# The state-to-output tables of a state-space layer, built beside the experts and no longer beside the linear attention

## Chip, cores and metric

One core of a Trainium2 chip. The metric is the time of one execution in device microseconds. Engines: TensorE (PE: matmuls; PEld: its weight loads), VectorE (DVE), ScalarE (ACT), GpSimd (POOL), SyncE (SP, which here only issues transfers). Sixteen DMA engines serve the queues of SP, ACT and POOL.

## What is computed

A first block (attention, an mLSTM, then a mixture of 32 experts, two per token) and a second block of two layers (gated linear attention, then a state-space layer "S5"), on 256 tokens of width 1024. The part that matters here is the output side of S5: a complex linear recurrence per group, of which the real part of C times the state is read.

```python
def step(carry, u_i):
    ...
    acum_r, acum_i, x_r, x_i = lax.associative_scan(_linrec_combine, (a_r, a_i, bu_re, bu_im), axis=1)
    ...
    y = jnp.einsum('bcgp,ghp->bcgh', x_r, c_re) - jnp.einsum('bcgp,ghp->bcgh', x_i, c_im)
```

The kernel takes four time steps at once. So it needs, beside C itself, the products C·A, C·A², C·A³ and C·A⁴ for each of 128 groups with 64 states: these are the state-to-output tables. They depend on weights alone.

## The kernel before

**Stages in time.** Modulation and first block to about 235 us; experts (`moe`) to 772; linear attention (`gla`) to 1070; S5 (`s5`) to the end.

**Experts.** `moe` runs eight calls of `quad`, four experts each. A call takes 24 tiles of weights of 1 MB (`w1`, `w3`, `w2`) from memory, through a pool of 5 and one of 2 buffers. `quad` yields after each tile, and `beside` steps two other jobs in between, at fixed rates: `kvs` (keys and values of the memory attention for both layers: 16 blocks of 1 MB) and `tables`.

**High and low halves.** Most dense products take each 1 MB block of fp32 weights in two halves. For each, ACT writes the rounded `whi` (L267), and another engine subtracts it from the raw block to give `wlo` (L268). In the experts that is POOL (`self.spread = 2`), later DVE. The raw buffer is free for SP's next load (L262) only when both are through with it.

**Tables.** `tables` first runs `s5_setup` (DVE: powers of A; POOL: clears of a few tiles, and zeros to parts of `tab3` in memory). Then it takes eight blocks `jb`: `s5_powers` makes B-side powers on DVE (24 products and sums of 128x128, lines 1285 to 1290) and copies C into block-diagonal tiles on POOL (L1304, L1306); one block later `s5_table` multiplies them on TensorE and POOL stores the result to `tab3` in four transfers (L1325).

**State-to-output tables.** `s5_out` loads C (`raw`, L1331), negates its imaginary part (L1335), and makes four complex products in turn, each from the one before: 24 elementwise instructions of 128x128 on POOL (lines 1339 to 1344). The result `t2` is stored to `tab2` in memory (L1346), from where S5 reads it long after, about 1300 us. In the trace `t2` and `s_t2` are shown as `s_t`, `tab2` and `tab3` as `tab`. It is called eight times in `gla`, in the loop over output blocks.

**Order.** Each engine works through its own queue in order. The queue isn't in program order: when the kernel is built, a planner walks through it with estimated durations, and gives each engine what is ready, earlier in the program first. `tc.issue_after(x)` keeps what is traced under it behind `x` on its engine. A tile of a pool has a name and a number of buffers; a new tile of that name waits until the last user of the old one is done. `s_tmp`, a 128x128 scratch tile, has one buffer in the pool of the tables (used by `s5_powers`), and one in the pool that `s5_out` used in `gla`.

Of the kernel before, what the change touches and what calls it, by code (L numbers as in the profile page):

```python
# [181 lines left out]
def bc(ap, n):  # L182

    return ap[:, None, :].to_broadcast([ap.shape[0], n, ap.shape[1]])
# [23 lines left out]
class Kern:  # L208
# [822 lines left out]
    def moe(self):  # L1031
        tc = self.tc
        with tc.tile_pool(name="moe", bufs=1) as R:
            W = tc.alloc_tile_pool(name="quad", bufs=2)
            self.lam = self.t(R, [128, 192], "lam")
            self.nc.gpsimd.dma_start(self.lam, self.io["slam"])
            steps = self.route(R)
            next(steps)
            xg = self.gather(0, W, "at")
            for _ in steps:  # L1040
                pass
            self.spread = 2
            for _ in range(4 * KV_EARLY):
                next(self.kvs)
            self.psum_banks(m=2, A=4, ps=2)
            self.kvtag = "ps"
            self.next = xg, None
            beside(self.quad(0, W), [(self.kvs, KV_FIRST)])
            self.pre.release()
            P = tc.alloc_tile_pool(name="aux", bufs=1, side="right")  # L1050
            self.kvpool, self.kvbufs = P, 4
            tables = self.tables(P)
            next(tables)
            for q in range(1, 8):
                if q == 7:
                    for _ in itertools.chain(self.kvs, tables):
                        pass
                    P.release()
                    self.overflow()
                    self.G = tc.alloc_tile_pool(name="gh", bufs=1, side="right")  # L1060
                beside(self.quad(q, W), [] if q == 7 else [(self.kvs, KV_LATER), (tables, TABLES)])
            W.release()
# [3 lines left out]
    def tables(self, P):  # L1066

        self.s5_setup(P)
        yield
        pair = [None, None]  # L1070
        for jb in range(9):
            if jb < 8:
                pair[jb % 2] = yield from self.s5_powers(P, jb)
            if jb:
                yield from self.s5_table(P, jb - 1, pair[(jb - 1) % 2])


    def memory(self, P):
# [91 lines left out]
    def s5_setup(self, P):  # L1170
# [4 lines left out]
        def f(name):  # L1175
            return self.t(P, [128, 64], "s_" + name)
# [13 lines left out]
        dt, a, b = f("dt"), f("a"), f("b")  # L1190
# [57 lines left out]
        for b in range(2):  # L1248
            p = self.psum()
# [10 lines left out]
        for x in self.bdC[0] + self.bdC[1]:  # L1260
            nc.gpsimd.memset(x, 0.0)

        zero = self.t(P, [48, 128], "s_zero")
        nc.gpsimd.memset(zero, 0.0)
        for k in range(3):
            n = 16 * (3 - k)
# [60 lines left out]
    def s5_out(self, P, jb):  # L1327

        nc, e = self.nc, self.nc.gpsimd
        raw = self.t(P, [128, 2, 8, 16], "s_raw", bufs=2)  # L1330
        e.dma_start(raw, self.io["sbc"][jb][:, 2:4])  # L1331
        t2 = self.t(P, [128, 8, 64, 2], "s_t2", bufs=2)
        tmp = self.t(P, [128, 8, 16], "s_tmp")
        A = [self.s5ab[:, i, 8 * jb:8 * jb + 8, None].to_broadcast([128, 8, 16]) for i in range(2)]
        e.tensor_scalar(raw[:, 1], raw[:, 1], -1.0, None, op0=OP.mult)  # L1335
        y = (raw[:, 0], raw[:, 1])
        for k in range(4):
            o = tuple(t2[:, :, 16 * k:16 * k + 16, i] for i in range(2))
            e.tensor_mul(o[0], y[0], A[0])
            e.tensor_mul(tmp, y[1], A[1])  # L1340
            e.tensor_add(o[0], o[0], tmp)
            e.tensor_mul(o[1], y[1], A[0])
            e.tensor_mul(tmp, y[0], A[1])
            e.tensor_sub(o[1], o[1], tmp)
            y = o
        e.dma_start(self.tab2[jb], t2.rearrange("p j s i -> p j (s i)"))  # L1346
# [19 lines left out]
    def gla(self):  # L1366
        nc, io, tc = self.nc, self.io, self.tc
        G0 = self.G
        with tc.tile_pool(name="g", bufs=1) as P, tc.tile_pool(name="gw", bufs=2) as W, \
# [27 lines left out]
            start = nc.gpsimd.tensor_mul(mg[:, 0:2, 0], rc, r1c)  # L1397
# [28 lines left out]
            a = self.t(P, [128, 4, T], "gA")  # L1426
# [87 lines left out]
            late = []  # L1514
            for b in range(12):
                ps = self.dense_t(io["gz"][b], h)
                if b < 8:
                    with tc.issue_after(start.ins):
                        self.s5_out(O, b)
                zt = self.t(W, [128, 2, T], "zt")  # L1520
                nc.vector.tensor_mul(zt, ps, bc(r, 2))
                nc.scalar.activation(zt, zt, AF.Silu)
                fs = (2 * b, 2 * b + 1)
                late.append([(f, self.gated(W, oh[f // 4][:, f % 4] if f < 16 else xa[:, f - 16], zt[:, f % 2])) for f in fs])
                for b_ in range(max(b - 1, 0), 12 if b == 11 else b):
                    for w, (f, y) in zip(self.halves(io["wo0"][b_]), late[b_]):
                        self.wout(acc, w, y, f == 0, f == 23)
                    if b == 10:
                        self.mark = self.last
# [258 lines left out]
```

## Time and profile before

| | |
|---|---|
| median of 3 runs (lowest to highest) | 1544.42 us (1543.29 to 1549.2) |
| the profiled execution | 1552.19 us, span 1550.4 us |
| busy: PE, DVE, ACT, POOL | 1353.3, 768.4, 549.9, 402.5 us |
| bytes moved by the DMA engines | 406.47 MB, mean 262 GB/s |
| POOL's own DMA queue | 9.54 MB, 1.8% of 16 engines' span |

The profile is one execution. Times are microseconds from the start of its span. "Busy" is the time in which an engine executes; "DMA share" is the mean busy share of the sixteen DMA engines, PEclk the TensorE clock that was granted, as a part of full speed. An arrow in a row reads "out <- in", and an arrow in brackets names what ended the wait.

### The profile page before, as it was taken

What the parts mean: (1) busy time and instruction counts of PE and PEld (TensorE: products, weight loads), DVE (VectorE), ACT (ScalarE), POOL (GpSimd) and SP (SyncE); (2) the same over time, 40 slices, a digit from 0 to 9 for tenths busy, and PEclk for the clock granted to TensorE, in tenths of its full rate; (3) what the DMA queues carried; (4) which work ended last, traced back from release to release, by engine and by line L of the source; (5) the groups of instructions that cost most, each with busy time, mean ns of one, the idle gap of its engine ahead of it and who ended that gap; (6) DMA issues with size and microseconds to landing.
All of it is one profiled execution on the core that took longest, in us unless ns stands there. A gap on an engine that the chain in (4) does not pass through costs nothing.

```text
span 1550.4 us, 25869 instructions
## 1 busy us (share of the span) xinstructions
PE 1353.3 (87%) x10632; PEld 1078.5 (70%) x10632; DVE 768.4 (50%) x1526; ACT 549.9 (35%) x861; POOL 402.5 (26%) x461
## 2 busy tenths in 40 slices
PE   6999989878897789766698999999789768899998
PEld 3777886434454455411198899999778767899998
DVE  2766464621143200100177765667646799755453
ACT  3754553122111212110145446545122354444443
POOL 0031032221332221100069970002334334330001
PEclk8999999998798989887888999999999989999998
DMA  9777666999999999998974444556686333565540
GB/s 376 263 257 263 259 227 253 373 407 418 413 401 395 421 417 403 418 420 366 401 259 161 148 155 170 182 187 205 192 220 186 121 113 109 181 201 184 174 160 28
DMA packets 84235, 406.47 MB, mean 262 GB/s; under 512 B 25088, under 2 KB 26672, under 8 KB 40080
## 3 DMA queue, kind: packets, MB, share of 16 engines
q1 hardware_dynamic: 67856, 386.04, 66.3%
q10 hardware_dynamic: 12720, 9.18, 1.8%
q0 software_dynamic: 3536, 9.54, 1.8%
q8 instruction: 86, 1.41, 0.4%
q14 instruction: 37, 0.30, 0.1%
HBM read 388.70 MB, written 16.02 MB: 261 GB/s over the span
## 4 chain that ended last, share of the span: by engine, by line
PE 33%; DVE 10%; DMA 9%; issue 1%; POOL 1%; ACT 0%; SPq 0%; DVEq 0%; POOLq 0%; ACTq 0%
PE ps L280 19%; PE acc L280 8%; DMA sm<-md 4%; DMA w<-in_w 3%; PE st L280 3%; DVE sc L1665 2%; DVE Xs L1668 2%; PE at L280 1%; DVE sc L1667 1%; DVE sc L1666 1%; PE A L280 1%; DMA yy<-yd 1%; PE m L280 0%; DVE zt L1576 0%; DVE wlo L268 0%
## 5 line engine op out<-in xcount | busy, mean ns | idle before, releaser
L267 ACT ACTIVATE whi<-w 128x1024 fp32r<-128x1024 f32 x252 | 263.1, 1054 | 341.9 <-PE ps L280 250.5
L268 DVE TENSOR_TENSOR wlo<-w,whi 128x1024 fp32r<-128x1024 f32 x198 | 258.2, 1307 | 150.8 <-ACT whi L267 150.3
L280 PE MATMUL ps<-hh,whi 128*128 128x256 f32 x928 | 278.2, 300 | 15.0 <-DVE zt L1576 6.2
L280 PE MATMUL ps<-hl,whi 128*128 128x256 f32 x928 | 271.2, 292 | 0.7 <-DVE hl L1541 0.4
L280 PE MATMUL ps<-hh,wlo 128*128 128x256 f32 x928 | 270.5, 292 | 0.0
L280 PEld LDWEIGHTS ps<-hh,whi 128*128 128x128 f32 x928 | 183.0, 197 | 23.5 <-issue 11.1
L268 POOL TENSOR_TENSOR wlo<-w,whi 128x1024 fp32r<-128x1024 f32 x54 | 129.0, 2398 | 255.5 <-ACT whi L267 255.4
L280 PEld LDWEIGHTS ps<-hl,whi 128*128 128x128 f32 x928 | 183.7, 198 | 2.0 <-DVE hl L1541 0.5
L280 PEld LDWEIGHTS ps<-hh,wlo 128*128 128x128 f32 x928 | 183.2, 198 | 1.6 <-issue 0.7
L280 PE MATMUL A<-w,xg 128*32 128x512 f32 x984 | 140.9, 674 | 34.1 <-DMA w<-in_w 33.2
L280 PE MATMUL acc<-gyl,whi 128*128 128x256 f32 x384 | 108.8, 284 | 1.6 <-DVE gyl L268 1.6
L280 PE MATMUL acc<-gyh,wlo 128*128 128x256 f32 x384 | 108.7, 283 | 0.0
L280 PE MATMUL acc<-gyh,whi 128*128 128x256 f32 x384 | 108.2, 283 | 0.0
L933 DVE SCALAR_TENSOR_TENSOR xT<-m,mod,xT 128x256 f32<-128x256 f32 x64 | 27.8, 480 | 146.7 <-PE m L280 146.7
L280 PE MATMUL A<-w,gT 128*32 128x512 f32 x512 | 74.9, 680 | 25.2 <-DMA w<-in_w 18.0
L280 PEld LDWEIGHTS A<-w,xg 128*32 128x32 f32 x984 | 23.8, 114 | 101.8 <-DMA w<-in_w 71.9
L280 PEld LDWEIGHTS acc<-gyl,whi 128*128 128x128 f32 x384 | 72.9, 190 | 2.4 <-DVE gyl L268 2.1
L280 PEld LDWEIGHTS acc<-gyh,wlo 128*128 128x128 f32 x384 | 73.2, 191 | 0.2 <-issue 0.2
L280 PEld LDWEIGHTS acc<-gyh,whi 128*128 128x128 f32 x384 | 72.6, 190 | 0.2 <-issue 0.2
L959 DVE TENSOR_TENSOR g<-g,A 128x512 f32<-128x512 f32 x8 | 5.5, 688 | 135.0 <-PE A L280 135.0
L280 PE MATMUL ps<-wlo,hh 128*128 128x256 f32 x192 | 55.9, 291 | 4.6 <-DVE wlo L268 4.6
L280 PE MATMUL ps<-whi,mh 128*128 128x256 f32 x128 | 43.3, 339 | 15.7 <-ACT whi L267 15.7
(577 smaller groups left out, 2791.0 us busy)
## 6 DMA issues: line engine op xcount, KB each, us to landing
w<-in_w SPq DMA_DIRECT2D x187, 1024.0 KB, 11.0
w<-in_wada SPq DMA_DIRECT2D x24, 1024.0 KB, 7.0
w<-in_wo SPq DMA_DIRECT2D x24, 1024.0 KB, 5.1
w<-in_sglu SPq DMA_DIRECT2D x16, 1024.0 KB, 4.9
w<-in_gz SPq DMA_DIRECT2D x12, 1024.0 KB, 4.9
w<-in_sz SPq DMA_DIRECT2D x12, 1024.0 KB, 4.9
w<-in_win SPq DMA_DIRECT2D x10, 1024.0 KB, 10.0
w<-in_xk SPq DMA_DIRECT2D x8, 1024.0 KB, 13.0
```

The lines of the kernel that those rows point to most:

```text
L267: self.nc.scalar.activation(hi, src, AF.Copy)
L268: (eng or self.nc.vector).tensor_sub(lo, src, hi.bitcast(F32))
L280: self.nc.tensor.matmul(ps, l, r, start=start, stop=stop, **kw)
L933: self.nc.vector.scalar_tensor_tensor(self.xT[:, f], pc[:, T * c:T * c + T], self.m(5)[:, f:f + 1], self.xT[:, f], op0=OP.mult, op1=OP.add)
L959: nc.vector.tensor_mul(g1, g1, p3)
L1665: nc.vector.tensor_mul(t1, Xs[:, :, c - 1], a4[0])
L1666: nc.vector.tensor_mul(t2, Xs[:, :, c - 1, ::-1], a4[1])
L1667: nc.vector.tensor_add(t1, t1, Xs[:, :, c])
L1668: nc.vector.tensor_add(Xs[:, :, c], t1, t2)
```

## The change

`s5_out` is called from `tables`, for block `jb - 1` directly behind that block's `s5_table`, and no longer from `gla`. It then uses the pool of the tables. The tiles `raw` and `t2` have one buffer each and no longer two, `raw` has a name of its own (`s_rawc`), and `s_tmp` is shared with `s5_powers`. The cleared tile of `s5_setup` takes its place in `s_tmp`'s buffer.

```diff
@@ tables
             if jb:
                 yield from self.s5_table(P, jb - 1, pair[(jb - 1) % 2])
+                self.s5_out(P, jb - 1)
@@ s5_setup
-        zero = self.t(P, [48, 128], "s_zero")
+        zero = self.t(P, [128, 8, 16], "s_tmp").rearrange("p a b -> p (a b)")[:48]
         nc.gpsimd.memset(zero, 0.0)
@@ s5_out
-        raw = self.t(P, [128, 2, 8, 16], "s_raw", bufs=2)
+        raw = self.t(P, [128, 2, 8, 16], "s_rawc")
         e.dma_start(raw, self.io["sbc"][jb][:, 2:4])
-        t2 = self.t(P, [128, 8, 64, 2], "s_t2", bufs=2)
+        t2 = self.t(P, [128, 8, 64, 2], "s_t2")
         tmp = self.t(P, [128, 8, 16], "s_tmp")
@@ gla
                 ps = self.dense_t(io["gz"][b], h)
-                if b < 8:
-                    with tc.issue_after(start.ins):
-                        self.s5_out(O, b)
```

## Rows read from the trace of the kernel before

**Rows 1.** The page's busy tenths: DMA, the span in 40 slices.

```profile
...
DMA  9777666999999999998974444556686333565540
...
```

**Rows 2.** Experts by stretch: span, busy PE, PEld, DVE, ACT, POOL, PEclk, DMA share.

```profile
...
300.00:320.00 20.00, 16.64 (x120) 7.78 (x112) 4.02 (x9) 7.02 (x16) 0.28 (x1) 1.00 0.88 356
...
520.00:540.00 20.00, 17.16 (x138) 8.98 (x134) 8.51 (x29) 4.84 (x11) 4.53 (x9) 1.00 1.01 421
...
680.00:705.00 25.00, 17.65 (x80) 4.66 (x84) 2.44 (x5) 1.19 (x2) 0.17 (x2) 0.66 0.82 334
...
```

**Rows 3.** Chain of waits, end of the experts: start us, us, what.

```profile
...
734.81 15.54 DMA w<-in_w
...
```

**Rows 4.** Linear attention by stretch, same columns.

```profile
...
785.00:818.00 33.00, 32.49 (x251) 31.17 (x251) 21.34 (x30) 12.20 (x14) 26.14 (x46) 0.94 0.65 234
818.00:839.00 21.00, 16.50 (x140) 16.29 (x138) 19.25 (x26) 15.32 (x19) 20.27 (x29) 0.95 0.24 82
839.00:875.00 36.00, 35.41 (x319) 34.62 (x320) 21.49 (x39) 14.47 (x23) 34.54 (x60) 0.94 0.60 212
875.00:893.00 18.00, 14.88 (x73) 11.79 (x72) 17.95 (x34) 7.92 (x18) 17.11 (x36) 1.00 0.27 96
893.00:930.00 37.00, 36.64 (x283) 36.24 (x284) 23.28 (x31) 16.20 (x19) 27.65 (x50) 0.95 0.47 161
...
```

**Rows 5.** DMA queues, 785 to 950 us: queue, packets, MB, share of 16 engines.

```profile
...
q0 software_dynamic: 1536, 5.24, 8.4%
...
```

**Rows 6.** DMA queues and issues (KB, us to landing), 262 to 600 us.

```profile
...
q1 hardware_dynamic: 17746, 129.24, 92.8%
q0 software_dynamic: 1952, 4.20, 4.1%
...
w<-in_w SPq DMA_DIRECT2D x112, 1024.0 KB, 10.8
...
tab<-s_zero POOLq DMA_DIRECT2D x2, 192.0 KB, 7.8
...
```

**Rows 7.** Timeline of DVE, start of the tables: start us, us, instruction.

```profile
...
284.00 0.28 DVE L1289 TENSOR_TENSOR s_tmp<-s_pe,a 128x128 f32<-128x128 f32 x1
284.31 2.32 DVE L1290 TENSOR_TENSOR s_pe<-s_pe,s_tmp 128x128 f32<-128x128 f32 x1
...
```

**Rows 8.** Timeline of POOL, the same place.

```profile
...
284.05 4.81 POOL L268 TENSOR_TENSOR wlo<-w,whi 128x1024 fp32r<-128x1024 f32 x2
...
```

**Rows 9.** Timeline of DVE, linear attention.

```profile
...
830.49 1.49 DVE L1444 SCALAR_TENSOR_TENSOR gqk<-gqk,gG 128x1024 f32<-128x1024 f32 x1
...
833.25 0.45 DVE L1448 TENSOR_SCALAR gqx<-gqk,gG 128x64 f32<-128x64 f32 x1
...
834.94 0.24 DVE L1450 TENSOR_SCALAR gqx<-gqk,gG 128x64 f32<-128x64 f32 x1
...
837.54 5.56 DVE L268 TENSOR_TENSOR wlo<-w,whi 128x1024 fp32r<-128x1024 f32 x4
...
880.15 2.30 DVE L1501 SCALAR_TENSOR_TENSOR gqk<-gqk,vec,gro 128x256 f32<-128x256 f32 x4
...
```

**Rows 10.** DVE by line and shape, 990 to 1070 us: busy, mean ns.

```profile
...
L268 DVE TENSOR_TENSOR wlo<-w,whi 128x1024 fp32r<-128x1024 f32 x28 | 34.3, 1225 | 26.0 <-ACT whi L267 26.0
...
L1360 DVE TENSOR_TENSOR gy<-hf,zt 128x256 f32<-128x256 f32 x8 | 3.0, 420 | 0.0
...
```

**Rows 11.** Timeline of DVE, third table's powers.

```profile
...
335.67 0.29 DVE L1285 TENSOR_TENSOR s_pe<-s_raw,s_co 128x128 f32<-128x128 f32 x1 [19.68 <-PE ps L280]
...
341.70 0.29 DVE L1286 TENSOR_TENSOR s_tmp<-s_raw,s_co 128x128 f32<-128x128 f32 x1
...
```

**Rows 12.** Timeline of POOL, the same table.

```profile
...
340.11 0.58 POOL L1278 DMA_DIRECT2D s_raw<-in_sbc  x1
353.69 4.67 POOL L268 TENSOR_TENSOR wlo<-w,whi 128x1024 fp32r<-128x1024 f32 x2 [13.00 <-ACT whi L267]
...
```

**Rows 13.** Waits of SP's queue, 262 to 700 us: total us, times, longest.

```profile
...
SPq L262 <- POOL wlo L268: 68.0, 12, 7.4
...
```

## Prediction, made before the change was run

> **What bounds the kernel now.** I read the busy tenths of the span first, then tables of stretches, then the waits and queues of the two stages that the change touches. The strip of transfers [rows 1] stands at its ceiling from slice 7 to slice 19 (some 270 to 770 us): these are the experts. The table of stretches says the same in numbers [rows 2]: between 300 and 600 us the DMA share is 1.01, while TensorE is busy 17 of 20 us. Two stretches fall short, 300 to 320 (0.88) and 680 to 705 (0.82). At the end of the stage the chain of waits is made of weight transfers, one of 15.5 us alone [rows 3]. So the experts last as long as their bytes need on 16 engines, and a byte added there is paid in time, unless it falls in one of the gaps.
>
> The linear attention (785 to 1070 us) is the other way round. Transfers take half of the engines or less, and TensorE is busy nearly all the time [rows 4]. It has two stretches of its own kind: 818 to 839 and 875 to 893, where DVE is busy 19.25 of 21 and 17.95 of 18 us and TensorE waits. In these DVE sets the pace, and POOL is full with `s5_out` beside it. Idle time of TensorE from 785 to 930, over the five rows: 0.5 + 4.5 + 0.6 + 3.1 + 0.4 = 9.1 us. That is all that a faster DVE can give back there.
>
> **What the change moves.** Eight calls of `s5_out`, each a load of 128 KB, 25 elementwise instructions on POOL and a store of 512 KB. POOL is busy 26.1 + 20.3 + 34.5 + 17.1 + 27.7 = 125.7 us in those five rows, nearly all of it this: 15.7 us a call. All of it goes to the experts.
>
> *Transfers.* 8 x (128 + 512) KB = 5.24 MB, the whole of POOL's queue in the linear attention: 8.4% of the engines over 165 us, 13.9 us of all sixteen [rows 5]. There the engines have room, so leaving costs and gives nothing. In the experts the shares of the queues already add up to the ceiling (92.8 and 4.1% for the two largest in rows 6), and these 13.9 us come on top. Bounds: at the rate of the full stage (421 GB/s, 520 to 540 in rows 2) 12.4 us; at the rate of what POOL's queue moves there now, 4.20 MB in 4.1% of 338 us, or 303 GB/s, 17.3 us [rows 6]. Those are smaller pieces, so I keep the time measured for these very transfers: **+13.9 us**.
>
> *DVE in the linear attention.* POOL and DVE get in each other's way when both read two operands from SBUF. Early in the experts a DVE product takes 0.28 us, the next 2.32 us: a POOL subtraction of 2.4 us began at 284.05 [rows 7, 8]. `s5_out` does this in small pieces. In the two DVE stretches [rows 9] a 1024-wide instruction with two inputs takes 1.4 us (5.56 for four; 1.49 alone), against 1.225 where POOL is idle [rows 10]: 11 of them, 0.17 each, 1.9 us. Twelve `gqx` scalings run from 833.25 to 837.54, 4.3 us; at the shortest of them, 0.24, they would need 2.9: 1.4 us. Twelve normalisations of the heads take 0.575 (2.30 for four), against 0.42 for a product of that width: 1.9 us. Together **-5.2 us**, all in stretches where TensorE waits for DVE. Bounds: nothing, if ScalarE or TensorE ends the wait next; 9.1 us, TensorE's whole idle time.
>
> The Trainium skill ("SBUF — State Buffer", the bandwidth-pool section) puts it as an exclusive lock: the one that starts second waits for the whole instruction of the other. The 2.32 us agree; the 0.17 us do not look like a whole POOL instruction each time. By the rule 23 two-input DVE instructions would each win back up to one POOL instruction, which is more than TensorE's idle time; what that makes of the time is the second rival below.
>
> *POOL and DVE in the experts.* `s_tmp` has one buffer. The trace shows how it is passed on: in the third call of `s5_powers` DVE works from 335.67, after table matmuls, and at 341.70 has begun the next call's first product into `s_tmp` [rows 11], though the rest of that call comes a table later. With `s5_out` in between, the planner, which takes what is ready and stands earlier in the program, must alternate: powers, out, powers, out. So one `s5_out` falls into each table's period of some 31 us, and they don't pile up. It can start at 341.7. The next POOL work after the table's own is a pair of subtractions (the low halves of the memory's key or value weights) at 353.7, 13.0 us after the issue before it [rows 12]. A call of 15.7 us, less without DVE beside it, ends up to 3 us too late. Behind it wait the two subtractions, the matmuls that need them, and SP's next load, which needs their source buffer: SP has waited 68 us for POOL in 12 places already [rows 13], without a gap in the transfers. What hides it: a load takes 10.8 us from issue to landing [rows 6] and so some four are always under way. I cost it at nothing; without that cover it is 8 x 3 = 24 us. DVE's first product of the next call also waits for `s_tmp`, and with it what stands behind it on DVE (expert gating, gathers, combines). It is issued late enough by the plan if the plan's times hold; same cover.
>
> The cleared tile, now in `s_tmp`'s buffer, holds back the first `s5_powers` until its transfers land (7.8 us, rows 6), once: nothing, by the same cover, 7.8 without it. Single buffers for the raw table and the result cost nothing, since a period is longer than load, 15.7 us and store.
>
> **Sum.** 13.9 - 5.2 = +8.7 us. The profiled execution took 1552.2 us (span 1550.4), 7.8 above the median of the runs shown, so it would become 1560.9, and the median 1544.4 becomes **1553**. With the bounds of the two terms: 12.4 - 9.1 = +3.3 to 17.3 - 0 = +17.3, so 1548 to 1562.
>
> **Rivals.**
> 1. *POOL becomes late.* If the planned order puts a whole `s5_out` ahead of the subtractions or of DVE work that TensorE needs, each costs what exceeds the cover: 15.7 - 10.8 = 4.9 us, eight times 39, on top of 8.7: 1592. It decides from the point where a subtraction comes over 10.8 us late. For: SP already waits for POOL [rows 13]. Against: the 13.0 us gap nearly holds a call.
> 2. *The lock gives back more.* All of TensorE's 9.1 us returns: 13.9 - 9.1 = +4.8, 1549. For: rows 7 and 8. Against: the small excess of rows 9 over 10.
> 3. *The transfers are hidden anyway* (the other side). If writes to memory run beside the reads, or fall into the gaps of 300 to 320 and 680 to 705, only the gain stays: -5.2, 1539, and with all of TensorE's idle time 1535. For: the two gaps hold 2.4 + 4.5 = 6.9 us. Against: the share of 1.01, and that `s5_out` would run between 300 and 600, mostly where there is no gap.
>
> **Chances.** Forecast 0.55, rival 1 0.18, rival 2 0.15, rival 3 0.12. About 0.5%, 7.7 us, is what a measurement of this kernel can tell from no change: beyond 1552 is slower, below 1537 faster. The forecast's range has a little over half beyond 1552: slower 0.36 + 0.18 = 0.54. Same: 0.19 + 0.15 + half of rival 3 = 0.40. Faster: the rest of rival 3, 0.06. The range: below 1543 lies most of rival 3, above 1575 most of rival 1, some 2 in 10 together, so 1543 to 1575.
>
> **What would show it.** Right: the experts' end (now 772) about 14 us later, at an unchanged DMA share near 1.0; POOL empty from 785 to 1070; the stretch 785 to 930 about 5 us shorter, its 1024-wide DVE instructions near 1.23 us; one `s5_out` behind each table, 25 instructions in 13 to 16 us. Wrong: new idle time of TensorE behind POOL's subtractions, or DVE standing at `s_tmp<-s_raw` for many us, with the DMA share well under 1 between 300 and 600 (rival 1); an expert stage no longer than before (rival 3); or several `s5_out` calls in one period. The step I trust least is the costless wait at `s_tmp`: the order on POOL and DVE is the planner's, and the trace of before can't show it.

## The result, and the profile after

The changed kernel takes 1601.67 us (median of four, 1600.53 to 1607.47) against 1545.29 for the kernel before on the same chip: 56.4 us more, a ratio of 1.0369 with a 95% interval of 1.0337 to 1.0402. The forecast was 1553; the first rival had 1592.

**Where the time is.** By the chain of waits, the first dense block of the linear attention starts at 776.82 us before and 840.40 after (+63.6). Its last block ends at 1070.35 before, and after at 1114.97 + 11.52 = 1126.49, so the linear attention takes 286.1 us where it took 293.5 (-7.4). The state-space layer behind it takes 479.2, before 480.05. Together +55.3, the difference of the two spans. Everything was lost in the experts.

The page's busy tenths after, first POOL, then DMA [rows 1]:

```profile
...
POOL 0041032533555544110000000000434433320001
...
DMA  9776657989998977999995425455777423474540
...
```

POOL's digits in slices 7 to 15 are 3 to 5 (on the page of before 1 to 3), and none stands in the linear attention (slices 21 to 27). The strip of transfers, before a row of nines from slice 7 to 19 with one 8, now has 8 in slices 8 and 12 and 7 in 14 and 15, all among the slices in which POOL is busier, and is whole again once POOL has next to nothing left to do. The tables of stretches say it in numbers. Columns as in [rows 2]; the experts and the linear attention of the kernel before:

```profile
262.00:776.80 514.80, 409.66 (x2756) 210.41 (x2749) 121.63 (x387) 89.19 (x168) 102.72 (x117) 0.86 0.99 403
776.80:1070.35 293.55, 284.32 (x2232) 276.22 (x2233) 195.11 (x295) 146.24 (x205) 126.10 (x218) 0.97 0.52 181
```

and the same of the kernel after, with two stretches of 20 us inside the experts:

```profile
262.00:840.40 578.40, 422.71 (x2769) 215.95 (x2761) 118.94 (x387) 89.46 (x168) 192.34 (x333) 0.81 0.92 368
300.00:320.00 20.00, 13.53 (x69) 7.09 (x67) 1.88 (x6) 1.72 (x4) 11.17 (x27) 0.75 0.88 347
600.00:620.00 20.00, 9.09 (x49) 6.23 (x50) 0.00 (x0) 0.00 (x0) 12.34 (x21) 0.57 0.37 138
840.40:1126.50 286.10, 283.01 (x2251) 274.88 (x2251) 186.47 (x300) 148.13 (x210) 1.75 (x5) 0.98 0.49 170
```

Before, the sixteen transfer engines taken together stood idle for 1% of 514.8 us, 5 us. After it is 8% of 578.4, 46 us: 41 us of the 63.6 are added idle time of the transfer engines. The other 22 are more busy time, of which the moved transfers make 13.8. That number is from POOL's queue in the table of DMA queues: 2.5% of 547 us before (230 to 777), 4.5% of 610 us after (230 to 840).

```profile
q0 software_dynamic: 3488, 9.44, 4.5%
```

About 8 us of busy time are left over; shares of two digits leave some 3 us open on either side of them.

**What POOL does at a table.** The timeline of POOL after, from the load of a table's raw block (the answer to [rows 12]):

```profile
355.84 0.56 POOL L1279 DMA_DIRECT2D s_raw<-in_sbc  x1
357.46 0.40 POOL L1341 TENSOR_TENSOR s_tmp<-s_rawc,a 128x128 f32<-128x128 f32 x1 [1.06 <-DVE s_pe L1291]
...
368.15 0.60 POOL L1347 DMA_DIRECT2D tab<-s_t  x1 [0.30 <-POOL s_t L1345]
374.33 0.40 POOL L1340 TENSOR_TENSOR s_t<-s_rawc,a 128x128 f32<-128x128 f32 x1 [5.58 <-DMA tab<-s_t]
374.69 0.39 POOL L1343 TENSOR_TENSOR s_t<-s_rawc,a 128x128 f32<-128x128 f32 x1
375.06 4.67 POOL L268 TENSOR_TENSOR wlo<-w,whi 128x1024 fp32r<-128x1024 f32 x2
```

Read the last four lines. A call of `s5_out` ends with its store at 368.15. Directly behind it in POOL's queue stand two products, not of this call but of the next one: they write the result tile `s_t`, which has one buffer, so they wait for the store to land (5.58 us). Only behind them come the subtractions that make `wlo`. These start 17.6 us after the call's first product into `s_tmp` (357.46), and 19.2 us after the load's issue, where before it was 13.6. The last two calls run one after the other:

```profile
589.57 0.62 POOL L1347 DMA_DIRECT2D tab<-s_t  x1 [0.30 <-POOL s_t L1345]
...
597.83 0.40 POOL L1340 TENSOR_TENSOR s_t<-s_rawc,a 128x128 f32<-128x128 f32 x1 [6.97 <-DMA tab<-s_t]
...
607.89 0.60 POOL L1347 DMA_DIRECT2D tab<-s_t  x1 [0.30 <-POOL s_t L1345]
608.50 4.69 POOL L268 TENSOR_TENSOR wlo<-w,whi 128x1024 fp32r<-128x1024 f32 x2
```

and TensorE stands until the subtraction is done, as its timeline shows:

```profile
610.91 0.58 PE L280 MATMUL ps<-wlo,mh 128*128 128x256 f32 x1 [20.91 <-POOL wlo L268]
```

This is the stretch 600 to 620 above: TensorE 9 of 20 us, DMA share 0.37. The matmuls wait for `wlo`, those of the experts stand behind them in TensorE's queue, their weight buffers don't come free, and SP can't issue the next loads.

**What DVE does at a table.** The timeline of DVE after, at the call that began at 357.46 on POOL:

```profile
367.89 0.29 DVE L1287 TENSOR_TENSOR s_tmp<-s_raw,s_co 128x128 f32<-128x128 f32 x1 [10.51 <-POOL s_t L1345]
368.10 0.68 DVE L959 TENSOR_TENSOR g<-g,A 128x512 f32<-128x512 f32 x1
```

and TensorE's:

```profile
368.83 0.90 PE L962 MATMUL m<-c_ident,g 128*128 128x128 f32 x3 [12.96 <-DVE g L959]
```

DVE stands for the whole call, with the first product of the next powers, at the one scratch tile. Right behind that product is `g`, the experts' gated activation, which TensorE needs next: it waits 12.96 us. The same pair stood there before; the row behind the one in [rows 11] is this, in the timeline of DVE of the kernel before:

```profile
342.51 0.69 DVE L959 TENSOR_TENSOR g<-g,A 128x512 f32<-128x512 f32 x1 [0.52 <-PE A L280]
```

**The waits of the experts after**, 262 to 760 us (engine, line, what for: total us, times, longest):

```profile
DVE s_tmp L1287 <- POOL s_t L1345: 59.8, 6, 10.6
...
POOL s_t L1340 <- DMA tab<-s_t: 52.2, 7, 9.6
...
PE ps L280 <- POOL wlo L268: 48.5, 11, 20.9
...
PE m L962 <- DVE g L959: 19.0, 6, 13.0
...
PE m L280 <- DVE xT L933: 12.9, 3, 5.9
```

The first two are the causes, the last three what TensorE has of them: 48.5 + 19.0 + 12.9 = 80.4 us. Before, it had 8.5 for `wlo`, 7.7 for `g` and nothing for `xT`, 16.2 in all. So TensorE stands 64.2 us more. SP's queue, where [rows 13] had 68.0 us in 12 places:

```profile
SPq L262 <- POOL wlo L268: 113.2, 12, 26.4
```

**The linear attention.** The timeline of DVE after, at the places of [rows 9]:

```profile
892.79 1.22 DVE L1445 SCALAR_TENSOR_TENSOR gqk<-gqk,gG 128x1024 f32<-128x1024 f32 x1
...
895.06 0.25 DVE L1449 TENSOR_SCALAR gqx<-gqk,gG 128x64 f32<-128x64 f32 x1
...
937.54 1.65 DVE L1502 SCALAR_TENSOR_TENSOR gqk<-gqk,vec,gro 128x256 f32<-128x256 f32 x4
```

With POOL gone, 1.49 became 1.22, the four normalisations 1.65 in place of 2.30, and the twelve scalings end 2.2 us after the first of them began (895.06 to 897.26), before 4.3.

### The profile page after: what moved, and what is told of

It is laid out like the page before. It is cut to its first block, busy times and chain, and to the rows that moved or that the text cites. A ratio compares the mean times of both kernels' runs of the same rounds, so it can differ in the third digit from the quotient of the medians.

```text
span 1605.7 us, 25868 instructions
## 1 busy us (share of the span) xinstructions
PE 1362.0 (85%) x10632; PEld 1082.6 (67%) x10632; DVE 755.0 (47%) x1526; ACT 550.5 (34%) x861; POOL 369.4 (23%) x461
## 4 chain that ended last, share of the span: by engine, by line
PE 33%; DVE 9%; DMA 7%; issue 1%; ACT 1%; POOL 0%; SPq 0%; DVEq 0%; POOLq 0%; ACTq 0%
PE ps L280 20%; PE acc L280 8%; DMA w<-in_w 3%; DMA sm<-md 2%; PE st L280 2%; DVE sc L1663 1%; DVE Xs L1666 1%; PE at L280 1%; DVE sc L1664 1%; DMA U<-ud 1%; PE A L280 1%; DVE wlo L268 1%; DVE sc L1665 1%; DMA yd<-U 0%; DMA yy<-yd 0%
## 5 line engine op out<-in xcount | busy, mean ns | idle before, releaser
L268 DVE TENSOR_TENSOR wlo<-w,whi 128x1024 fp32r<-128x1024 f32 x198 | 254.2, 1287 | 151.6 <-ACT whi L267 151.1
L280 PE MATMUL A<-w,xg 128*32 128x512 f32 x984 | 147.0, 702 | 29.3 <-DMA w<-in_w 28.4
L1541 POOL COPY xT<-u 128x256 f32<-128x256 f32 x8 | 7.4, 931 | 277.5 <-DVE u L1535 277.2
L280 PE MATMUL ps<-wlo,mh 128*128 128x256 f32 x128 | 40.9, 320 | 29.3 <-POOL wlo L268 29.3
```

The costliest lines, as they stand in the source:

```text
L268: (eng or self.nc.vector).tensor_sub(lo, src, hi.bitcast(F32))
L280: self.nc.tensor.matmul(ps, l, r, start=start, stop=stop, **kw)
L1541: nc.gpsimd.tensor_copy(self.xT[:, k], u)
```

## The experiments

Three things had to be told apart: what the bytes cost, what the linear attention gives back, and which wait in the experts costs the rest: POOL's subtractions behind a store, POOL's subtractions behind a call's own instructions, or DVE behind `s_tmp`. Each run is compared with the kernel before on its own chip, with a 95% interval of the ratio. "Costs" is the difference of the medians; the interval is 2 to 6 us wide on either side of it, so differences of a few us between runs lie within the noise.

**The bytes alone.** Kernel before, and per table one more load of 128 KB and one store of 512 KB on POOL's queue, from a cleared tile to memory that nothing reads.

```diff
                 yield from self.s5_table(P, jb - 1, pair[(jb - 1) % 2])
+                with self.tc.issue_after(self.tail.ins):
+                    self.s5_bytes(P, jb - 1)
+    def s5_bytes(self, P, jb):
+        ...
+        e.dma_start(raw, self.io["sbc"][jb][:, 2:4])
+        e.dma_start(self.tab2x[jb], self.t2z)
```

> The kernel before, with the transfers alone added to the experts: behind each table 128 KB are loaded and a cleared 512 KB tile is stored to memory that nobody reads; s5_out stays in the linear attention. If the transfers are paid in full there, the experts end 13.9 us later: 1545 + 14 = 1559, with the DMA share still 1.0. If the loss of the change is queueing alone and transfers are hidden, 1545 to 1548.

Measured: 1557.34 against 1544.21, 1.0076 [1.0051, 1.0100]: the bytes cost 13.1 us. Between 300 and 600 us (table of stretches) the share stays at the ceiling:

```profile
300.00:600.00 300.00, 244.14 (x1718) 139.91 (x1715) 69.92 (x207) 53.17 (x94) 85.49 (x99) 0.86 1.01 413
```

The transfers are paid in full, within the interval. The third rival, hidden transfers, falls.

**The linear attention without the products.** Kernel before; the 25 instructions of a call replaced by one clear, load and store kept.

```diff
-        e.tensor_scalar(raw[:, 1], raw[:, 1], -1.0, None, op0=OP.mult)
-        ...
+        e.memset(t2, 0.0)
         e.dma_start(self.tab2[jb], t2.rearrange("p j s i -> p j (s i)"))
```

> The kernel before, with the 25 products and sums of each s5_out left out (the tables become zeros: one clear of the tile per call); its loads and stores stay in the linear attention. If POOL's reads slow DVE there, the stage gets shorter by the 7.5 us by which it is shorter after the change: 1537.5. If that gain came from the transfers leaving the stage, 1545.

Measured: 1535.21 against 1544.21, 0.9939 [0.9919, 0.9959]: 9.0 us come back. The linear attention of this run, columns as in [rows 2]:

```profile
775.14:1059.28 284.14, 280.57 (x2232) 272.42 (x2233) 184.29 (x295) 146.22 (x205) 16.50 (x26) 0.98 0.53 187
```

Beside the row of before (293.55 us, TensorE 284.32 busy, clock 0.97) the stage is 9.4 us shorter: 5.6 are idle time of TensorE (9.2 before, 3.6 here), 3.8 are shorter busy time of TensorE, at a mean granted clock of 0.98 for 0.97. So the bytes and the linear attention together make +4.1 us, and 56.4 - 4.1 = 52.3 us are waits in the experts.

**Two buffers for the result.** Kernel after; the second buffer lies in the memory of a tile of the setup.

```diff
-        mt = self.t(P, [64, 2, 4, 2, 64], "s_mt")
+        mt = self.t(P, [128, 2, 4, 2, 64], "s_t2", bufs=2)[0:64]
...
-        t2 = self.t(P, [128, 8, 64, 2], "s_t2")
+        t2 = self.t(P, [128, 8, 64, 2], "s_t2", bufs=2)
```

> The changed kernel, with two buffers for the result tile of s5_out (the memory comes from a tile of the setup that shares them). Theory W, that POOL waits for the store to land with the subtractions queued behind: the 52 us of those waits go, and with them most of the new idle time of the transfers (41 us): 1602 - 30 = 1572, between 1562 and 1580. Theory S, that DVE's wait for the scratch tile is what costs: no change within 6 us, 1596 to 1602. If bytes alone cost: 1602.

Measured: 1574.52 against 1544.21, 1.0185 [1.0144, 1.0226], so it costs 30.3 us and not 56.4: without the wait for the store some 26 us are gone. Its waits, 262 to 760 us:

```profile
DVE s_tmp L1287 <- POOL s_t L1345: 62.5, 6, 12.1
...
PE m L962 <- DVE g L959: 19.3, 6, 13.4
...
PE ps L280 <- POOL wlo L268: 17.8, 6, 11.0
```

TensorE's wait for `wlo` has shrunk from 48.5 to 17.8, of which 11.0 is one wait behind the last two calls, which still run back to back. DVE's at `s_tmp` and TensorE's for `g` are as long as ever. 30.3 - 4.1 = 26.2 us of waits are left.

**No transfers in the experts.** Kernel after with C loaded once and no stores there; a cleared tile is stored from the linear attention.

```diff
+        if jb == 0:
+            self.rawc = self.t(P, [128, 2, 8, 16], "s_rawc")
+            e.dma_start(self.rawc, self.io["sbc"][jb][:, 2:4])
...
-        e.dma_start(self.tab2[jb], t2.rearrange("p j s i -> p j (s i)"))
```

> The changed kernel, whose s5_out in the experts computes but neither loads (but once) nor stores; zeros are stored to the table from the linear attention, so the tables are left out of the result. Takes away bytes and the wait for the store together, and leaves POOL's 25 instructions and DVE's wait for the scratch tile. If W and bytes are the loss (41 + 14 of 64 us): 1602 - 50 = 1552, at least below 1560. If POOL's instructions and DVE's waits are the loss: 1602 - 14 = 1588.

Measured: 1565.70 against 1547.14, 1.0119 [1.0097, 1.0141]. With no store to wait for and no byte moved it still costs 18.6 us, 27.6 with the 9.0 that the linear attention gives back: the 26 us again, from the other side, and a time between the two that were expected. I first took these for the time of POOL's own instructions ahead of its subtractions. That was wrong, as the two runs with the calls held behind their table show.

**A scratch tile of its own for `s5_out`.** Kernel after; DVE's powers and POOL's products no longer share a buffer. Beside it the same with two result buffers.

```diff
-        tmp = self.t(P, [128, 8, 16], "s_tmp")
+        tmp = self.t(P, [128, 8, 16], "s_m2")
```

> The changed kernel, with a scratch tile of its own for s5_out, so that DVE's powers and POOL's tables no longer take turns on one buffer. Theory S: the 60 us of DVE's waits (six, up to 10.6 us, the combines behind them) go, 1602 - 20 = 1582. Theory W: the waits for the store stay ahead of the subtractions, and calls of s5_out may follow one another more closely now, so 1595 or more, perhaps above 1602.

> The changed kernel with both: two result tiles and a scratch tile of its own. If waits W and S together make all of the loss beyond the bytes, 1545 + 14 - 7.5 = 1551 to 1555. If POOL's own 11 us per call ahead of the subtractions cost as well, more: up to 8 times what they exceed the loads under way, 1560 to 1575. If calls now follow one another without a pause, the subtractions between them come later still, and it may be as slow as 1600.

Measured: 1615.45 against 1544.21, 1.0463 [1.0423, 1.0502], a cost of 71.2 us; with both edits 1597.47 against 1547.14, 1.0310 [1.0281, 1.0340], 50.3 us. DVE's wait is gone, but the timeline of POOL with the scratch tile alone shows what came in its place (the stores of five calls):

```profile
305.97 0.60 POOL L1347 DMA_DIRECT2D tab<-s_t  x1 [0.30 <-POOL s_t L1345]
...
373.31 0.61 POOL L1347 DMA_DIRECT2D tab<-s_t  x1 [0.30 <-POOL s_t L1345]
...
383.48 2.34 POOL L268 TENSOR_TENSOR wlo<-w,whi 128x1024 fp32r<-128x1024 f32 x1
```

Nothing holds the next call back any more, and five of them (three stores between the two shown are left out) run without a subtraction between them, up to the one at 383.48. TensorE waited 55.78 us for it. So these two runs, meant to tell DVE's wait apart, don't: they take one wait away and bring a longer one.

**The subtractions on DVE.** Kernel after; from the second `quad` on DVE makes `wlo`, and POOL has only the tables. Beside it the same edit of the kernel before, as a control.

```diff
             P = tc.alloc_tile_pool(name="aux", bufs=1, side="right")
+            self.spread = 0
             self.kvpool, self.kvbufs = P, 4
```

> The changed kernel, with the low halves of the keys' and values' weights made by DVE from the second group of experts on, and no longer by POOL. If the loss is that they stand behind s5_out on POOL, it goes: 1602 - 30 = 1572 or less. But DVE waits up to 10.6 us for the scratch tile, and they may stand behind that: then 1590 and more.

> The kernel before, with the low halves of the keys' and values' weights made by DVE from the second group of experts on: the control for the run in which the changed kernel got the same edit and took 1555. If that run was fast because the subtractions no longer stood behind s5_out, this one is no faster than the kernel before: 1545, within 4 us. If DVE's subtraction (1.3 us, against 2.4 on POOL) helps the experts by itself, 1535 or less, and the 47 us of that run prove less.

Measured: 1555.17 against 1547.14, 1.0053 [1.0034, 1.0073]; the control 1544.53 against 1546.45, 0.9984 [0.9969, 1.0000]. The waits with this edit of the changed kernel, 262 to 760 us:

```profile
DVE s_tmp L1288 <- POOL s_t L1346: 54.3, 6, 10.6
...
POOL s_t L1341 <- DMA tab<-s_t: 50.5, 7, 8.7
```

Both waits are nearly as long as before, and the cost fell from 56.4 to 8.0 us. The edit changes the order on DVE too: TensorE now waits 7.5 us for `g` and 3.8 for `xT`, where it had 19.0 and 12.9. So what a wait of some 50 us on an engine costs depends on what stands behind it.

**Half a call.** The kernel without transfers, with two of the four complex products.

```diff
-        for k in range(4):
+        for k in range(2):
```

> The changed kernel without the transfers of s5_out in the experts (zeros are stored from the linear attention), and with two of its four complex products left out as well: 13 instructions per call, some 5.5 us. The run with all four took 1566, of which 1547 - 9 = 1538 would be left without POOL's time. If POOL's own time ahead of the subtractions is paid only beyond the loads under way, half a call costs nearly nothing: 1538 to 1545. If it is paid in proportion, half of 28: 1552.

Measured: 1538.42 against 1546.45, 0.9939 [0.9918, 0.9961]: 8.0 us faster, and with the 9.0 of the linear attention 1.0 us of waits where whole calls had 27.6. DVE's wait at `s_tmp` is half as long (30.0 us), and the cost is gone: it isn't in proportion.

**Calls held behind their table.** Two runs with POOL's queue in almost the same order: the products of a call stand behind the last store of its own table (the load may go earlier). No product of the next call stands ahead of the subtractions, and the last two calls are a table apart. They differ in the scratch tile: the last two lines of the diff belong to the second run alone.

```diff
-            nc.gpsimd.dma_start(dst[:n, :, k], t3[64 - n:])
+            self.tail = nc.gpsimd.dma_start(dst[:n, :, k], t3[64 - n:])
...
+        with self.tc.issue_after(self.tail.ins):
             t2 = self.t(P, [128, 8, 64, 2], "s_t2")
-            tmp = self.t(P, [128, 8, 16], "s_tmp")
+            tmp = self.t(P, [128, 8, 16], "s_m2")
```

> Changed kernel with one call of the state-to-output products held behind the last store of its own table on POOL (its load stays free to go earlier); the scratch tile is still shared with DVE. So no product of the next call stands ahead of the subtractions, and the last two calls are a table apart. Theory A (the waits in the experts have two places: POOL's subtractions behind a store, and DVE's first product of the next powers, which waits at the shared scratch tile for a whole call with TensorE's operands queued behind it): the first part goes, the second stays; TensorE still waits 5 to 13 us for DVE in two or three places; 1564 to 1574. Theory B (POOL's own instructions ahead of the subtractions are all that remains, DVE's wait is harmless): the same time as with a scratch tile of its own, the next run, within 5 us. If neither costs: bytes 13.1 less 9.0 of the linear attention, about 1550.

> The same, held behind the table, and with a scratch tile of its own: DVE no longer waits for a call, and POOL's queue stands in the same order as in the run beside it. Theory A: TensorE's waits for DVE (5 to 13 us each) are gone, 1548 to 1556, at least 10 us under the run beside it. Theory B: POOL's subtractions still come behind a whole call of 10.7 us at each table, so the time is within 5 us of the run beside it, near 1574 if the 26 us left over with two result buffers were POOL's own instructions.

Measured: with the shared tile 1575.15 against 1545.08, 1.0196 [1.0175, 1.0216], a cost of 30.1 us; with a tile of its own 1547.81, 1.0019 [1.0005, 1.0034], 2.7 us. The waits, 262 to 760 us, with the shared tile:

```profile
DVE s_tmp L1287 <- POOL s_t L1346: 73.0, 6, 15.0
...
PE m L962 <- DVE g L959: 24.0, 6, 15.1
...
PE m L280 <- DVE xT L933: 16.3, 2, 9.3
...
PE ps L280 <- POOL wlo L268: 7.9, 6, 2.0
```

and with its own:

```profile
PE m L962 <- DVE g L959: 9.3, 7, 2.5
...
PE ps L280 <- POOL wlo L268: 7.1, 5, 2.2
```

The scratch tile alone is worth 27.3 us here: theory A, and not B, which had the two within 5 us of each other. And POOL's own instructions cost nothing: whole calls stand ahead of the subtractions in both runs, and TensorE waits no longer for `wlo` than the 8.5 us of the kernel before. The timeline of POOL in the second shows why:

```profile
339.45 2.31 POOL L1326 DMA_DIRECT2D tab<-s_t  x4
341.84 0.52 POOL L1337 TENSOR_SCALAR s_rawc<-s_rawc 128x128 f32<-128x128 f32 x1
...
353.93 0.59 POOL L1348 DMA_DIRECT2D tab<-s_t  x1 [0.30 <-POOL s_t L1346]
354.55 4.68 POOL L268 TENSOR_TENSOR wlo<-w,whi 128x1024 fp32r<-128x1024 f32 x2
```

The call lies in what was POOL's idle gap of 13.0 us [rows 12], and fills it almost exactly.

**All of them beside each other.** TensorE's waits between 262 and 760 us, over the 16.2 of the kernel before, and what a run costs without the bytes (13.1) and the linear attention (-9.0), us. A cost carries the intervals of its own run and of the terms that are taken off:

| run | `wlo` | `g`, `xT` | over 16.2 | cost |
|---|---|---|---|---|
| after | 48.5 | 31.9 | 64.2 | 52.3 |
| two result buffers | 17.8 | 32.1 | 33.7 | 26.2 |
| no transfers | 18.0 | 28.4 | 30.2 | 27.6 |
| own scratch tile | 82.3 | 11.3 | 77.4 | 67.1 |
| both | 64.9 | 7.4 | 56.1 | 46.2 |
| subtractions on DVE | 4.3 | 11.3 | -0.6 | 3.9 |
| half a call | 7.3 | 13.6 | 4.7 | 1.0 |
| behind the table, shared | 7.9 | 40.3 | 32.0 | 26.0 |
| behind the table, own | 7.1 | 9.3 | 0.2 | -1.4 |

These waits of TensorE go with the cost in every run. In the six runs in which it stands 30 us longer or more, eight to nine tenths of that are paid, whichever engine it stands for; in the other three both numbers are within 5 us of nothing. A part of the rest can be seen in TensorE's wait for the weights themselves, over the whole stage, first before (262 to 776.8 us):

```profile
PE A L280 <- DMA w<-in_w: 51.2, 44, 4.9
```

and after (262 to 840.4 us):

```profile
PE A L280 <- DMA w<-in_w: 38.7, 35, 3.2
```

That fits loads that landed while TensorE stood for something else: the cover, 12.5 us of it. TensorE's busy time in the stage also rose, from 409.7 to 422.7 us, at a mean granted clock of 0.81 for 0.86. It isn't paid by itself: in the run of the table's last row TensorE is busy for 419.0 us of the experts, at 0.84, the share of the transfers is 0.99, and nothing is lost.

```profile
262.00:784.20 522.20, 419.00 (x2764) 211.79 (x2756) 126.64 (x387) 89.57 (x168) 193.67 (x333) 0.84 0.99 407
```

**The calls later in the linear attention.** Kernel before; the instruction behind which `s5_out` is issued moved from before the gates to behind the last head's normalisation.

```diff
-            start = nc.gpsimd.tensor_mul(mg[:, 0:2, 0], rc, r1c)
...
+            start = nc.gpsimd.tensor_copy(mg[:, 0:2, 0], oh[3][:, 3, 0:2])
```

> The kernel before, with s5_out in the linear attention, but let go only when the last head is normalised (some 898 us, and no longer 786), behind both stretches in which DVE sets the pace. If POOL's reads cost only there, the 7.5 us come back without the bytes: 1538. If DVE is slowed as much in what follows (940 to 1070 us), 1545; if the last table then comes late for the state-space layer, above.

Measured: 1536.09 against 1547.14, 0.9931 [0.9908, 0.9955], 11.1 us faster than the kernel before and so faster than both. The chain has the linear attention from 770.24 to 1054.92, 284.7 us, 8.8 shorter. One of its stretches with `s5_out`, later than any of [rows 4]:

```profile
950.00:970.00 20.00, 20.00 (x170) 20.00 (x169) 13.03 (x16) 10.94 (x14) 18.87 (x32) 1.00 0.73 249
```

POOL is as full as in [rows 4] and TensorE doesn't wait: DVE has 7 us to spare here.

**Later, and the subtractions on DVE.** Both edits on the kernel before.

> The kernel before with both edits that left it no slower: s5_out let go only after the last head is normalised, and the subtractions of the experts on DVE. If the edits are independent and the second is worth nothing, as for the late start alone: 0.993 of before, 1536. If it is worth some us, 1530 to 1535.

Measured: 1535.24 against 1546.45, 0.9931 [0.9913, 0.9949], the same as the move alone.

## Why the prediction was wrong, step by step

**The step that failed** is "POOL and DVE in the experts", which ends in "I cost it at nothing". Measured: 52.3 us. It failed at two sentences.

One is "Single buffers for the raw table and the result cost nothing, since a period is longer than load, 15.7 us and store". The period is long enough. But I asked when the next call can run, and not where its first instructions stand: two of them stood directly behind the store and ahead of the subtractions, and in an in-order queue the subtractions wait for a store that doesn't concern them. With two result buffers some 26 us are gone, and of TensorE's waits it is the one for `wlo` that shrinks, by 30.7 us.

The other is on DVE's first product at `s_tmp`: "It is issued late enough by the plan if the plan's times hold; same cover". It is issued early, and `g` and `xT`, which TensorE needs at once, stand behind it; the row behind the one in [rows 11] was such a `g`. With the calls held behind their table, sharing the tile costs 27.3 us more than not sharing it, and without the sharing no cost of waits is left (-1.4 us). In the changed kernel itself 24.2 of TensorE's 64.2 us of longer waits are of this kind. That the queues stand so is shown by the timelines; why the planner chose the order (it takes what it holds ready and stands earlier in the program) is argued, not shown.

**The cover** that I counted on, loads under way, is small: eight to nine tenths of TensorE's longer waits were paid. What does hide a call is POOL's own gap of 13 us up to the subtractions, which a call fits: 12.1 us from its first instruction to its store where calls are held behind their table and have a tile of their own (341.84 to 353.93), two issues of loads among them. I had it up to 3 us too long for the gap, at 15.7.

**The first rival** was the right one in its mechanism, "a whole `s5_out` ahead of the subtractions or of DVE work that TensorE needs", and near in size: 39 us against 52.3. Its working was not: 15.7 - 10.8 us eight times has neither the store nor `s_tmp` in it.

**The transfers** held: +13.9 foretold, 13.1 measured alone, 13.8 in POOL's queue.

**DVE in the linear attention** was right in its cause and too small: -5.2 foretold; -7.4 in the stage, -9.0 measured alone. The forecast counted only idle time of TensorE and took its 9.1 us for all that there was to gain. That the 9.0 come so near to this bound is luck. With the products left out 5.6 of 9.2 us of idle time returned, close to the 5.2; the other 3.8 us are shorter busy time of TensorE, at a mean granted clock of 0.98 for 0.97, a term that the forecast doesn't have. (After the change itself the stage lost 6.1 us of idle and 1.3 of busy time.) So the second rival, all of the idle time, is near in size and not in its working. The rule of the Trainium skill ("SBUF — State Buffer", section "SBUF: two separate sides"), that the instruction which starts first holds the shared pair of ports and the other one waits until it is through, had pointed to all of the idle time and more, if each wide instruction lost a whole one of POOL's. The rows don't show that much: single wide instructions got shorter by 0.27 us, where a product of POOL's took some 0.6 us, and 3.6 of the 9.2 us of idle time stayed.

**The alternation** of powers and calls at `s_tmp` came as foretold, except at the end, where no powers stand between the last two calls. "The step I trust least" was named rightly, and left in the sum at nothing. Whether the cleared tile in this buffer cost anything was not tried by itself. With both waits gone the change costs 2.7 us, 4.1 by its two measured terms, 8.7 by the forecast.

## What to carry to other kernels

When two engines share a single buffer, or one waits for a store, price the wait by what stands directly behind the waiting instruction in its queue, and look for that row in the timeline of before: waits of 54 us in all cost 4 us in one order, waits of 73 us cost 27 in another. A shared buffer can also be what keeps an order apart, so take it away together with a tie that does the same (own tile and tie: 2.7 us; own tile alone: 71.2). And work that nobody needs soon belongs where its engine and that engine's neighbour have room: a later place in the same stage gave 11.1 us.

## What was not expected of the hardware

The 25 elementwise instructions of a call kept POOL busy for 10.7 us in the experts (0.40 to 0.46 us a product), where DVE works little, and for 15.2 us in the linear attention of the kernel before, beside a busy DVE (means of eight calls, from the profiles' rows by line). So the interference seems to slow POOL as well as DVE; no run takes DVE's work away there, so this cause is argued and not shown. The same store of 512 KB took 8.3 us to land in the full experts and 4.7 in the linear attention (medians of eight each).
